# Reading neighbourhood values straight from the normed values, a lasting weight slot, and other queues and buffers at the turn from projection to scan

## The chip, the cores and the metric

The kernel runs on one core of a Trainium2 chip. The metric is the device time of one execution in microseconds (us); smaller is better. Before the change the median of three runs is 1549.68 us (1549.65 to 1550.4). The change is a set of edits around the moment at which the kernel goes from its input projection to its scan and attention.

## The reference

One layer of a hybrid backbone: 256 context tokens and 1024 latent tokens of width 1024. After a normalisation with learned shift and scale, one projection feeds two groups of heads. Group A is a gated DeltaNet: a five-tap convolution over the sequence and SiLU on q, k and v, and then a scan over chunks, forward and backward. Group B is an attention of every latent token to a window on a 2-D grid 64 wide, and to the context. Both go through one output projection, and a SwiGLU network follows. Cut to what the change touches:

```python
qkv = short_conv(p[..., :3 * DN_WIDTH], conv_w)          # convolution, then SiLU
q, k, v = split(qkv)                                      # DeltaNet, 4 heads of 128
z = p[..., 3 * DN_WIDTH:4 * DN_WIDTH]                     # output gate
o = rms_norm(scan_forward(q, k, v) + scan_backward(q, k, v)) * silu(z)
nq, nk, nv = na_qkv(p)                                    # attention, 8 heads of 64, q and k normed
# each latent query: one softmax over its window keys (12 grid rows x 32 columns a block)
# plus the 256 context keys; values are gathered from nv in the same window
```

## The kernel before

**Staging.** The projection is a list of jobs (L1030 to 1041) that all read the same 1280-token input, held in SBUF (on-chip memory) as pairs `hh`, `hl`. A Block job makes 128 output channels: 24 groups of three matmuls (L405) into three PSUM banks, a copy out by ScalarE (L453), the convolution on VectorE (L457 to 461), SiLU (L468), and a `finish` that norms, splits or transposes and stores to DRAM. A Wide job makes 256 channels with the tokens on the partitions (L595), its weights in a slot `zw`. The order is k0 to k3, z's second half (z1), nk0 to nk2, the first half of the attention's values (nv0), nk3, q0 to q3, nq0 to nq3, v0, nv1, v1 to v3, and z's first half (z0). Beside the jobs run background generators: the inverses of the chunks' triangular matrices, the preparation of chunks (`preps`, which stores `y_d` and `at_d`, L1010), and the modulation vectors. With z0 the attention begins (`fill`, L1064 to 1068); then scan and attention run interleaved, and after them the output projection and the feed-forward network.

**What sets the order.** An automatic scheduler orders the instructions of every engine at build time; at run time each engine takes them strictly in that order, and each waits for what it needs. DMAs are issued in the same in-order streams of SyncE (SP) or ScalarE (ACT). The framework gives the DMAs of a program a set of eight completion semaphores in turn, so an issue also waits until the DMA eight places before it has landed. Tiles live in stacks on the left and right of SBUF; a tile that is put over an older one waits for the last reader of the old one.

**What the change touches.**

- `values` (L276 to 281) loads for each of 32 attention pairs a tile `vw`, 192 KB, from `vw_d`. That DRAM tensor is a rearranged copy of `nv_d`, made after nv1 by 64 DMAs of 64 KB from DRAM to DRAM on SP (L1103 to 1109).
- `Block.finish` for v stores `vt` to `v_d` on SP (L535). The scan loads `v` from `v_d` (L1165).
- Wide jobs: z1, nv0 and nv1 take `zw` from the pool `zp`, which belongs to `late`, the pools that close before z0; z0 takes it from `sp1`, a new pool that is opened only once `late` is closed (L1061 to 1068). Each slot is filled in two halves through one landing tile `wraw`: load (L586), cast by ScalarE (L587), rest by GpSimd (POOL, L588). `sp1` later holds the scan's output `oacc` in the same slot.
- z0 gathers its gate tile `zg` (L624) under the tag `kx` of the pool `cp`, stores it by ACT's queue (L627).
- `norm` of nk and nq: per segment of tokens one matmul (L492) into a bank and one Ln by ScalarE (L493); nk has three segments. The bank comes from the tag `m`; the tag `pr` serves `preps`.
- `mneg`, two masks times -1e30, is made at the start of the kernel.
- The scan's pools on the right stack: `sl` (loads `kt`, `y`, `kT`, `qT`, `at`), then a pad, then `sw` (work tiles and `v`).

## Time and profile before

| | us |
|---|---|
| median of three runs | 1549.68 |
| the profiled execution's own time | 1549.54 |
| its span, first to last instruction | 1547.5 |
| TensorE (PE) busy | 1479.8 |
| VectorE (DVE) busy | 994.3 |
| ScalarE (ACT) busy | 727.7 |
| GpSimd (POOL) busy | 233.6 |
| mean granted TensorE clock | 0.982 |

Times in the trace are us from the start of the span. In a row of the timeline stand start, duration, engine, line, operation, output<-input, how many, and in brackets the idle time before it and what ended it. SPq and ACTq are the queues on which SP and ACT issue DMAs: such a row shows the time of issuing, not of the transfer. A row of the windows gives for a stretch its length, then busy time and instruction count of PE, PE's weight loads, DVE, ACT and POOL, then the granted TensorE clock, the mean busy share of the 16 DMA engines and GB/s.

### The profile page before, as it was taken

What the parts mean: (1) busy time and instruction counts of PE and PEld (TensorE: products, weight loads), DVE (VectorE), ACT (ScalarE), POOL (GpSimd) and SP (SyncE); (2) the same over time, 40 slices, a digit from 0 to 9 for tenths busy, and PEclk for the clock granted to TensorE, in tenths of its full rate; (3) what the DMA queues carried; (4) which work ended last, traced back from release to release, by engine and by line L of the source; (5) the groups of instructions that cost most, each with busy time, mean ns of one, the idle gap of its engine ahead of it and who ended that gap; (6) DMA issues with size and microseconds to landing.
All of it is one profiled execution on the core that took longest, in us unless ns stands there. A gap on an engine that the chain in (4) does not pass through costs nothing. (4 is left out here: it accounts for less than half of the span.)

```text
span 1547.5 us, 23963 instructions
## 1 busy us (share of the span) xinstructions
PE 1479.8 (96%) x8702; PEld 1235.2 (80%) x8702; DVE 994.3 (64%) x1712; ACT 727.7 (47%) x1404; POOL 233.6 (15%) x286
## 2 busy tenths in 40 slices
PE   6999999899989978999999999999999999999998
PEld 3788787678778867888887878888888888888887
DVE  5774497675554543777986469866665556599652
ACT  5442552635764235666773166333333334354440
POOL 1154500733554010111210000000000000000000
PEclk9999999999999979999999999999999999999999
DMA  9274221577556467899637502632323324698742
GB/s 389 64 217 133 67 72 63 163 212 241 182 169 212 130 174 237 283 288 261 220 102 255 208 34 82 211 102 103 103 102 103 109 100 159 231 381 279 244 144 82
DMA packets 204118, 267.35 MB, mean 173 GB/s; under 512 B 16736, under 2 KB 114528, under 8 KB 202976
## 3 DMA queue, kind: packets, MB, share of 16 engines
q1 hardware_dynamic: 198480, 261.07, 51.7%
q10 hardware_dynamic: 5520, 4.76, 0.9%
q8 instruction: 68, 1.11, 0.3%
q14 instruction: 50, 0.41, 0.1%
HBM read 201.02 MB, written 68.94 MB: 174 GB/s over the span
## 5 line engine op out<-in xcount | busy, mean ns | idle before, releaser
L405 PE MATMUL blk<-hh,whi 128*128 128x512 f32 (+1 forms) x410 | 123.4, 395 | 2.3 <-ACT kk L550 1.4
L1415 ACT CAST uhi<-wq 128x512 fp32r<-128x512 f32 x101 | 61.0, 622 | 133.5 <-issue 84.6
L1415 ACT CAST uhi<-ws 128x512 fp32r<-128x512 f32 x91 | 53.9, 621 | 147.3 <-PE ps L1354 92.9
L405 PE MATMUL blk<-hl,whi 128*128 128x512 f32 (+1 forms) x410 | 116.8, 377 | 0.3 <-DVE hl L707 0.3
L595 PE MATMUL blk<-zw,hh 128*128 128x256 f32 (+1 forms) x576 | 115.0, 293 | 1.3 <-ACT kk L550 1.1
L405 PE MATMUL blk<-hh,wlo 128*128 128x512 f32 (+1 forms) x410 | 114.7, 377 | 0.6 <-POOL wlo L200 0.6
L1416 DVE TENSOR_TENSOR ulo<-wq,uhi 128x512 fp32r<-128x512 f32 x101 | 67.4, 687 | 59.1 <-ACT uhi L1415 34.0
L1354 PE MATMUL ps<-hT,uhi 128*128 128x512 f32 x336 | 103.7, 390 | 0.0
L1354 PE MATMUL ps<-hT,ulo 128*128 128x512 f32 x336 | 103.5, 389 | 0.0
L1354 PE MATMUL ps<-lT,uhi 128*128 128x512 f32 x336 | 103.4, 389 | 0.0
L595 PEld LDWEIGHTS blk<-zw,hh 128*128 128x128 f32 x576 | 92.8, 192 | 5.2 <-ACT kk L550 1.4
L1354 PE MATMUL ps<-hB,uhi 128*128 128x512 f32 x288 | 89.2, 391 | 0.6 <-ACT hB L1529 0.6
L1354 PE MATMUL ps<-lB,uhi 128*128 128x512 f32 x288 | 88.7, 389 | 0.4 <-DVE lB L1530 0.4
L1354 PE MATMUL ps<-hB,ulo 128*128 128x512 f32 x288 | 88.7, 389 | 0.0
L405 PEld LDWEIGHTS blk<-hh,wlo 128*128 128x128 f32 x410 | 72.6, 192 | 15.3 <-POOL wlo L200 0.9
L405 PEld LDWEIGHTS blk<-hl,whi 128*128 128x128 f32 x410 | 72.4, 191 | 14.5 <-DVE hl L707 0.8
L405 PEld LDWEIGHTS blk<-hh,whi 128*128 128x128 f32 x410 | 69.4, 194 | 18.2 <-issue 4.5
L595 PE MATMUL blk<-zw,hl 128*128 128x256 f32 (+1 forms) x288 | 83.2, 289 | 0.0
L1354 PEld LDWEIGHTS ps<-lT,uhi 128*128 128x128 f32 x336 | 63.1, 188 | 13.1
L1354 PEld LDWEIGHTS ps<-hT,ulo 128*128 128x128 f32 x336 | 63.1, 188 | 13.1
L1354 PEld LDWEIGHTS ps<-hT,uhi 128*128 128x128 f32 x336 | 62.9, 188 | 13.0
L200 POOL TENSOR_TENSOR wlo<-wraw,whi 128x1024 fp32r<-128x1024 f32 x18 | 44.7, 2485 | 179.2 <-ACT whi L199 160.7
(359 smaller groups left out, 3540.5 us busy)
## 6 DMA issues: line engine op xcount, KB each, us to landing
wq<-w_fo SPq DMA_DIRECT2D x99, 256.0 KB, 4.2
wq<-w_gu SPq DMA_DIRECT2D x88, 256.0 KB, 2.9
wad<-wa SPq DMA_DIRECT2D x64, 256.0 KB, 4.4
bt<-rpb SPq DMA_DIRECT2D x64, 192.0 KB, 3.8
t_d<-g SPq DMA_DIRECT2D x22, 512.0 KB, 3.6
fr<-t_d SPq DMA_DIRECT2D x44, 256.0 KB, 5.0
f_d<-g SPq DMA_DIRECT2D x33, 256.0 KB, 2.1
fr<-f_d SPq DMA_DIRECT2D x33, 256.0 KB, 3.8
```

The costliest lines, as they stand in the source:

```text
L200: lo_engine.tensor_tensor(o, r, h.bitcast(F32), OP.subtract)
L405: pe.matmul(o, ww[:, k], xx[k][:, s], start=k == 0 and j == 0, stop=k == KT - 1 and j == 2)
L595: pe.matmul(p[:, :c1 - c0], x[k][:, s], ww[:, k, c0:c1], start=k == 0 and j == 0, stop=k == KT - 1 and j == 2)
L1354: pe.matmul(o, w[wi][:, k], x[xi][:, k], start=first and k == 0 and j == 0, stop=k == n - 1 and j == 2, skip_group_check=True)
L1415: act.copy(hi, self.raw[key])
L1416: dve.tensor_tensor(lo, self.raw[key], hi.bitcast(F32), OP.subtract)
```

## The change

Five edits:

1. The copy `nv_d` to `vw_d` goes. `values` reads `nv_d` itself, by four DMAs of 48 KB (32 partitions each, in pieces of 512 B) where it had one of 192 KB.
2. The four v blocks' stores to `v_d` go out on ACT's queue.
3. All four Wide jobs take `zw` from one slot of `sp1`, which is opened before `late`, and z0's weights can so be fetched like any other; `zg` takes the tag `cr` for `kx`.
4. The third segment of nk's norm takes its bank from `pr`; `mneg` moves to the pool `adp`, and its two multiplications behind the masks' arrival.
5. In the scan's right-hand stack `sw` now comes first, then the pad, then `sl`, and `v` is an `sl` tile; the loaded tiles thereby lie over the convolution's buffers.

```diff
@@ values, L276
             vw = nw.tile([128, 3, 128], F32, name="vw", tag="vw", bufs=3)
-            sp.dma_start(vw, vw_d[:, hp, cb, half:half + 3])
+            for r in range(4):
+                rows = nv_d[CT:].rearrange("(n r c) d -> r c n d", r=4, c=64)[r, BLKS[cb]:BLKS[cb] + 32, half:half + 3]
+                sp.dma_start(vw[r * 32:r * 32 + 32], rows[:, :, hp * 128:hp * 128 + 128])
@@ Block.norm, L490
-                for s0, n in self.segs:
-                    p = bank()
+                for j, (s0, n) in enumerate(self.segs):
+                    p = bank("pr" if j == 2 else "m")
@@ Block.finish, L535
-                    sp.dma_start(dst[:, i * 128:(i + 1) * 128].rearrange("(c p) d -> p c d", p=128), vt)
+                    (act if kind == "v" else sp).dma_start(dst[:, i * 128:(i + 1) * 128].rearrange("(c p) d -> p c d", p=128), vt)
@@ Wide, L574
-                w = self.zp().tile([128, 2, KT, 256 if self.lasting else 272], F32R, name="zw", tag="zw")
+                w = sp1.tile([128, 2, KT, 272], F32R, name="zw", tag="zw")
-                if not self.lasting:
-                    self.room()
+                self.room()
-                            zg = cp.tile([128, NCH, 128], F32, name="zg", tag="kx", bufs=3)
-                            zg = zg.rearrange("p a b -> p (a b)")[:, :1024]
+                            zg = cp.tile([128, T], F32, name="zg", tag="cr", bufs=2)
+                            zg = zg[:, :1024]
@@ masks and pools, L756
-                        for d in range(2):
-                            act.mul(mneg[:, d], masks[:, d], -1.0e30)
+        sp1 = pools(middle, "sp1", "left")
         adp = pools(late, "adp", "left")
-        zpool = [pools(late, "zp", "left")]
+        mneg = adp.tile([128, 2, 128], F32R, name="mneg", tag="mneg")
+        for d in range(2):
+            act.mul(mneg[:, d], mr[:, d].bitcast(F32), -1.0e30)
@@ before z0, L1061
                 late.close()
-                sp1 = pools(middle, "sp1", "left")
-                zpool[0] = sp1
-                jobs[n + 1].room()
@@ after nv1, L1103
-            if isinstance(j, Wide) and n == values:
-                vlat = nv_d[CT:].rearrange("(r c) d -> r c d", c=64)
-                for cb in range(4):
-                    for ch in range(4):
-                        for r in range(4):
-                            sp.dma_start(vw_d[r * 32:r * 32 + 32, :, cb, ch],
-                                         vlat[4 * ch + r, BLKS[cb]:BLKS[cb] + 32].rearrange("c (h d) -> c h d", d=128))
@@ scan, L1143
-        sl = pools(gs, "sl", "right", 3)
+        sw = pools(gs, "sw", "right", 2)
         shift(gs, "spad", "right", 16)
-        sw = pools(gs, "sw", "right", 2)
+        sl = pools(gs, "sl", "right", 3)
@@ load, L1164
-                t = work(name, 3) if name == "v" else sl.tile([128, 4, 128], F32, name=name, tag=name)
+                t = sl.tile([128, 4, 128], F32, name=name, tag=name)
```

The edits also make the scheduler order the engines anew. Three places of that order follow; a row holds line (the change's lines lie 2 to 4 above those of before in this region, 14 in the scan), operation, output<-input, shape and count.

**From the last chunks to the start of z0.** SP before: `vw_d` is the copy, `at_d` and `y_d` the last chunks' stores, `wraw<-w_z` the two halves of z0's weights, `qs`, `kh`, `kl`, `vc`, `bt` and `vw` the attention's loads.

```order
L1108 DMA vw_d<-nv_d 128x128 x53
L1010 DMA at_d<-at 128x512 x2
L1010 DMA y_d<-y_2229 128x512
L1010 DMA y_d<-y_2230 128x512
L1010 DMA y_d<-y_2231 128x512
L1010 DMA y_d<-y_2232 128x512
L586 DMA wraw<-w_z 128x8x128
L535 DMA v_d<-vt 128x10x128
L260 DMA qs<-nq_d 128x1024
L262 DMA kh<-nk_d 64x1280
L263 DMA kl<-nk_d 64x1280
```

SP with the change:

```order
L1006 DMA at_d<-at 128x512 x2
L1006 DMA y_d<-y_2228 128x512
L1006 DMA y_d<-y_2229 128x512
L584 DMA wraw<-w_z 128x8x128
L1006 DMA y_d<-y_2231 128x512
L1006 DMA y_d<-y_2230 128x512
L584 DMA wraw<-w_z 128x8x128
L258 DMA qs<-nq_d 128x1024
L260 DMA kh<-nk_d 64x1280
L261 DMA kl<-nk_d 64x1280
L260 DMA kh<-nk_d 64x1280
L261 DMA kl<-nk_d 64x1280
```

The 53 copies are gone, the second half of the weights is issued ahead of the attention's loads and not 15 rows behind the first, and no store of `v_d` stands between. PE there, before: the end of v3 (L405) and the first rows of the attention (L303, scores of the first pair).

```order
L405 MATMUL blk<-hh_458,wlo 128x256
L405 MATMUL blk<-hh_458,wlo 128x512 x2
L303 LDWEIGHTS qs
L303 MATMUL sc<-kh,qs 128x256
L303 LDWEIGHTS qs
L303 MATMUL sc<-kh,qs 128x256
```

PE with the change:

```order
L405 MATMUL blk<-hh_456,wlo 128x256
L405 MATMUL blk<-hh_456,wlo 128x512 x2
L593 MATMUL blk<-zw,hh_127 128x256
L593 MATMUL blk<-zw,hl_128 128x256
L593 MATMUL blk<-zw,hh_127 128x256
L593 MATMUL blk<-zw,hh_129 128x256
L593 MATMUL blk<-zw,hl_130 128x256
```

z0's matmuls (L593) now follow v3 directly. Past 96 matmuls of it come the transposes for v's store and only then the first scores:

```order
L593 MATMUL blk<-zw,hl_457 128x256
L593 MATMUL blk<-zw,hh_456 128x256
L527 MATMUL m<-cst,cacc 128x128 x4
L303 LDWEIGHTS qs
L303 MATMUL sc<-kh,qs 128x256
L303 LDWEIGHTS qs
L303 MATMUL sc<-kl,qs 128x256
```

**The third segment of nk3.** PE before (L492 is the norm's matmul; the L405 rows ahead of it end the block q0, those behind belong to q1):

```order
L405 MATMUL blk<-hl_459,whi 128x512 x2
L405 MATMUL blk<-hh_458,wlo 128x512 x2
L492 MATMUL m<-cr,cst 128x256
L492 MATMUL m<-cr,cst 128x512
L405 MATMUL blk<-hh_129,whi 128x512 x2
L405 MATMUL blk<-hl_130,whi 128x512 x2
L492 MATMUL m<-cr,cst 128x512
L405 MATMUL blk<-hh_129,wlo 128x512 x2
```

PE with the change; the third matmul doesn't follow the second:

```order
L405 MATMUL blk<-hl_457,whi 128x512 x2
L405 MATMUL blk<-hh_456,wlo 128x512 x2
L492 MATMUL m<-cr,cst 128x256
L492 MATMUL m<-cr,cst 128x512
L405 MATMUL blk<-hh_127,whi 128x512 x2
L405 MATMUL blk<-hl_128,whi 128x512 x2
L405 MATMUL blk<-hh_127,wlo 128x512 x2
```

It comes 87 rows on, behind the last rows (L994) of the first two chunks' preparation, whose banks have the same tag, and within q2:

```order
L994 MATMUL pr<-y_2230,kk 32x96
L994 MATMUL pr<-y_2231,kk 32x96
L994 MATMUL pr<-y_2230,kk 32x96
L994 MATMUL pr<-y_2231,kk 32x96
L405 MATMUL blk<-hh_454,whi 128x512 x2
L405 MATMUL blk<-hl_455,whi 128x512
L492 MATMUL pr<-cr,cst 128x512
L405 MATMUL blk<-hl_455,whi 128x512
L405 MATMUL blk<-hh_454,wlo 128x512 x2
```

**The last store of v.** ACT before, from the last copy out of z0 (L624) to the attention's next copies; SP issues the store of v3 meanwhile:

```order
L624 COPY zg<-blk 128x256
L626 ACT_TABLE_LOAD
L626 ACTIVATE zg<-zg 128x1024
L317 COPY pt<-sc 128x640
L627 DMA z_d<-zg 128x4x256
L317 COPY pt<-sc 128x640
L307 ACT_TABLE_LOAD
L307 ACTIVATE bt,mx<-bt,mx 128x640 x2
L326 COPY no<-sc 128x8x16
```

ACT with the change:

```order
L622 COPY zg<-blk 128x256
L624 ACT_TABLE_LOAD
L624 ACTIVATE zg<-zg 128x1024
L317 COPY pt<-sc 128x640
L625 DMA z_d<-zg 128x4x256
L317 COPY pt<-sc 128x640
L307 ACT_TABLE_LOAD
L307 ACTIVATE bt,mx<-bt,mx 128x640 x2
L535 DMA v_d<-vt 128x10x128
L326 COPY no<-sc 128x8x16
```

The store of `v_d` stands behind the silu of z's gate, a table load and two exponentials of the attention.

More of the change, by code (lines that the diff above doesn't have):

```diff
@@ L137, in hybrid @@
     mr = const("mr", [128, 5, 128], F32R)
-    mneg = const("mneg", [128, 2, 128], F32R)
     v_d = dram.tile([T, 512], F32, name="v_d", tag="v_d")
@@ L149, in hybrid @@
     nk_d = dram.tile([2, NAH, ND, T], F16, name="nk_d", tag="nk_d")
-    vw_d = dram.tile([128, 4, 4, 4, 128], F32, name="vw_d", tag="vw_d")
     y_d = dram.tile([2, NCH, 128, 4, 128], F32, name="y_d", tag="y_d")
@@ L564, in hybrid, with __init__ @@
         class Wide:
-            def __init__(self, kind, half, zp):
-                self.kind, self.half, self.zp = kind, half, zp
+            def __init__(self, kind, half):
+                self.kind, self.half = kind, half
                 self.n = 272 if kind == "z" and half else 256
-                self.lasting = kind == "z" and not half
             def room(self):
-                w = self.zp().tile([128, 2, KT, 256 if self.lasting else 272], F32R, name="zw", tag="zw")
+                w = sp1.tile([128, 2, KT, 272], F32R, name="zw", tag="zw")
                 self.hi, self.lo = w[:, 0], w[:, 1]
@@ L767, in hybrid @@
         KKc = WK[:, 1]
-        def zp():
-            return zpool[0]
         def decay_tables(gp):
@@ L1028, in preps @@
                 flush(tick[0] + 2)
-        jobs = first + [Block("k", 2), Block("k", 3), Wide("z", 1, zp)]
+        jobs = first + [Block("k", 2), Block("k", 3), Wide("z", 1)]
         inv = len(jobs)
-        jobs += [Block("nk", i) for i in range(3)] + [Wide("nv", 0, zp), Block("nk", 3)]
+        jobs += [Block("nk", i) for i in range(3)] + [Wide("nv", 0), Block("nk", 3)]
         turn = len(jobs)
@@ L1036, in hybrid @@
         queries = range(turn, later)
-        jobs += [Block("nq", i) for i in range(4)] + [Block("v", 0), Wide("nv", 1, zp)]
+        jobs += [Block("nq", i) for i in range(4)] + [Block("v", 0), Wide("nv", 1)]
         values = len(jobs) - 1
-        jobs += [Block("v", i) for i in (1, 2, 3)] + [Wide("z", 0, zp)]
+        jobs += [Block("v", i) for i in (1, 2, 3)] + [Wide("z", 0)]
         def blk(n):
@@ L1142, in hybrid @@
     with ExitStack() as gs:
+        sw = pools(gs, "sw", "right", 2)
+        shift(gs, "spad", "right", 16)
         sl = pools(gs, "sl", "right", 3)
-        shift(gs, "spad", "right", 16)
-        sw = pools(gs, "sw", "right", 2)
         gs.callback(scan_psum.close)
```

## The prediction

> **What bounds the kernel now.** I read the page first, then the windows around the places where PE idles, then PE's waits there, and last the queue that feeds them. The page says that PE is nearly always busy, and that the chain that ended last is PE's:
>
> ```profile
> span 1547.5 us, 23963 instructions
> PE 1479.8 (96%) x8702; PEld 1235.2 (80%) x8702; DVE 994.3 (64%) x1712; ACT 727.7 (47%) x1404; POOL 233.6 (15%) x286
> ...
> PE 41%; DVE 1%; issue 0%; DVEq 0%
> ```
>
> So 1547.5 - 1479.8 = 67.7 us are PE's idle time, and an edit that removes no matmul can win only from these and from matmuls that ran at a lower granted clock. The windows show where (length, then busy time of PE, PEld, DVE, ACT, POOL, the clock, DMA share, GB/s):
>
> ```profile
> 200.00:258.00 58.00, 52.48 (x348) 46.34 (x346) 55.62 (x56) 23.29 (x34) 5.46 (x2) 1.00 0.22 64
> ...
> 258.00:300.00 42.00, 37.79 (x184) 30.20 (x183) 25.71 (x21) 22.96 (x39) 22.42 (x27) 0.87 0.54 182
> 300.00:344.00 44.00, 40.63 (x261) 32.55 (x259) 28.44 (x30) 20.01 (x35) 15.70 (x15) 0.89 0.53 159
> ...
> 495.88:531.97 36.09, 36.09 (x262) 29.20 (x261) 14.06 (x20) 12.66 (x26) 4.68 (x9) 1.00 0.38 112
> ...
> 548.50:563.38 14.88, 3.93 (x19) 2.24 (x19) 12.70 (x17) 6.63 (x10) 2.57 (x2) 0.63 1.06 294
> 563.38:569.50 6.12, 5.98 (x29) 5.50 (x28) 3.05 (x6) 2.03 (x5) 2.39 (x2) 0.51 0.50 139
> 569.50:595.04 25.54, 25.49 (x218) 24.38 (x217) 4.55 (x9) 8.12 (x14) 0.31 (x1) 1.00 0.36 98
> 595.04:607.16 12.12, 8.57 (x60) 6.69 (x58) 6.13 (x13) 10.25 (x15) 0.93 (x3) 0.72 1.01 308
> ...
> 600.00:800.00 200.00, 194.47 (x1824) 171.28 (x1825) 151.80 (x461) 142.31 (x389) 33.40 (x68) 0.98 0.81 251
> 820.00:1547.50 727.50, 722.24 (x3198) 596.55 (x3196) 471.38 (x745) 288.35 (x488) 0.00 (x0) 1.00 0.47 160
> ```
>
> From 820 on PE lacks 5 us of 727, and the change edits nothing there: what is won or lost before 820 goes to the end at full value. The one deep hole lies between the last matmul of v3 (548.5) and the first of z0 (563.38). What PE waited for from 545 to 610, and when z0 began, ended and the scan's first product ran:
>
> ```profile
> PE sc L303 <- DVE mx L305: 5.1, 2, 4.1
> PE sc L303 <- DMA kh<-nk_d: 4.5, 1, 4.5
> PE sc L314 <- DVE bt L309: 3.0, 2, 2.3
> ...
> 563.38 0.56 PE L595 MATMUL blk<-zw,hh 128*128 128x256 f32 x1
> ...
> 595.04 0.38 PE L527 MATMUL m<-cst,cacc 128*128 128x128 f32 x2
> ...
> 607.16 1.13 PE L1217 MATMUL ps<-v,y 128*128 128x128 f32 x8 [0.66 <-DMA y<-y_d]
> ```
>
> The causes stand in SP's queue:
>
> ```profile
> 495.88 36.09 SPq L1108 DMA_DIRECT2D vw_d<-nv_d  x53
> 532.07 1.01 SPq L1010 DMA_DIRECT2D at_d<-at  x2
> 533.18 2.42 SPq L1010 DMA_DIRECT2D y_d<-y  x4
> 535.68 0.61 SPq L586 DMA_DIRECT2D wraw<-w_z  x1
> 545.47 0.37 SPq L535 DMA_DIRECT2D v_d<-vt  x1
> 545.93 0.63 SPq L260 DMA_DIRECT2D qs<-nq_d  x1
> ...
> 555.34 0.60 SPq L586 DMA_DIRECT2D wraw<-w_z  x1
> ...
> 596.43 0.39 SPq L535 DMA_DIRECT2D v_d<-vt  x1
> ...
> 602.13 0.32 SPq L1165 DMA_DIRECT2D v<-v_d  x1
> ```
>
> The 53 copies keep SP for 36 us; then the store of v1 waits until 545.47 for its data with the attention's loads right behind it, and the second half of z0's weights comes last, at 555.34. So PE has neither scores nor z0 to work on. It waits 4.5 us for `kh`, 4.1 us for the first pair's bias step, which stands on DVE behind v3's convolution, and 2.3 us for the pair's softmax.
>
> **The change part by part. The hole before z0** (edits 1 to 3). With the copies and the v store out of SP's stream, the second half of z0's weights is issued behind the last chunks' stores and needs its landing tile only. I put it near 530, since nothing but those chunks holds it, instead of 555.34; the lasting slot removes the wait for the pools' closing. In PE's order z0 follows v3 directly, and 96 matmuls of it run before the first scores, which gives DVE time for v3's convolution. What can be recovered: idle 14.88 - 3.93 = 10.95, 6.12 - 5.98 = 0.14 and 25.54 - 25.49 = 0.05, so 11.1 us; slow clock 3.93 x (1 - 0.63) = 1.5 and 5.98 x (1 - 0.51) = 2.9, so 4.4 us. Together 15.5 us. Against it stand new waits, which this trace doesn't show: z0's first bank is released by ScalarE's copies of v3, at most the 1.35 us of the first row below; the two casts of z0's weights now stand around v2's copies in ScalarE's order and may hold the banks of v2, at most two of the second row, 2.1 us; and the first pair's softmax may keep PE for the 2.3 us that it takes now. Each may as well be 0, since z0 leaves PE other work. I take half of their 5.8, 2.9 us: **12.6 us won**, between 9.7 and 15.5.
>
> ```profile
> 548.13 1.35 ACT L453 COPY cr<-blk 128x256 f32<-128x256 f32 x3 [5.77 <-PE blk L405]
> 549.35 1.07 ACT L587 CAST zw<-wraw 128x1024 fp32r<-128x1024 f32 x1
> ```
>
> **nk's third segment** (edit 4). Four waits for the bank, and the times of nk3's third Ln and of the last copy (L1001) of the first two chunks' preparation:
>
> ```profile
> PE m L492 <- ACT cr L493: 5.3, 4, 1.4
> ...
> 274.51 0.69 ACT L493 ACTIVATE cr<-m,bias 128x512 f32<-128x512 f32 x1 [0.64 <-PE m L492]
> ...
> 320.43 0.47 ACT L1001 COPY y<-pr 32x384 f32<-32x384 f32 x1 [2.14 <-PE pr L998]
> ```
>
> Two of the waits lie in 200 to 258, where DVE is busy 55.62 of 58 us: the inverses' chain on DVE takes up what PE gains there. The other two are worth 2.7 us. But for nk3 the order shows the third product behind those chunks' preparation, so its Ln goes from 274.5 to about 320, and ACT loads its tables twice more. Behind it queue nk3's Exp, its store, and the release of its tiles to q0's squares and q1's convolution. Who waits? The sums and products of q0 and q1, which the order moves back; PE gets the blocks q2 and q3 instead. From 258 to 344 there are 4.2 + 3.4 = 7.6 us idle before. Upper bound: 2.7 and half of that, 6 us won. Lower bound: the pushed-back products find no cover and cost as much as half the idle time and two table loads (1.28 us each by the row below), about 5 us lost with the two waits not regained. I take **2 us won**, nearer the gain, because PE's own matmuls need nothing from nk3.
>
> ```profile
> 595.63 1.28 ACT L626 ACT_TABLE_LOAD   x1
> ```
>
> **The scan's start** (edits 2 and 5). The loads over the convolution's buffers no longer wait for z0's last matmul, but that wait decides nothing before: the first load, `v`, waits for v3's store (596.43, `v` at 602.13), and `kt`, `y`, `kT` are queued behind it. The store now stands on ACT behind the last silu, the store of z, two copies, a table load and two exponentials. By the trace of those same instructions, which run from 595.24 to 602.98 before, it goes out some 7 us after the end of z0's last products where it took 1.4, so the first scan product comes up to 18 us behind them, not 12.1. PE has more of the attention to run meanwhile: in its order 8 us of products stand ahead of the first scan row against 5, at the durations that they have at full clock, 3 us more. That is 5.6 - 3 = 2.6 us lost; if ACT gets there early, as its casts and copies now lie further ahead, 3 us are won of the 12.12 - 8.57 = 3.6 idle and 8.57 x 0.28 = 2.4 slow. I take **1.5 us lost**, nearer the queue's arithmetic.
>
> ```profile
> 595.24 0.37 ACT L624 COPY zg<-blk 128x256 f32<-128x256 f32 x1 [2.76 <-PE blk L595]
> ...
> 602.98 0.19 ACT L307 ACTIVATION_READ_ACCUMULATOR bt<-bt,mx 128x1 f32 x1
> ```
>
> **Four loads for one** (edit 1). 32 loads become 128, so 96 more issues and the same 6.3 MB, in 600 to 800:
>
> ```profile
> bt<-rpb SPq DMA_DIRECT2D x64, 192.0 KB, 3.8
> ...
> vw<-vw_d SPq DMA_DIRECT2D x32, 192.0 KB, 3.6
> ...
> 640.44 0.32 SPq L278 DMA_DIRECT2D vw<-vw_d  x1
> ...
> 679.29 0.35 SPq L1165 DMA_DIRECT2D y<-y_d  x1
> ```
>
> Each costs SP at least the 0.32 us above: 96 x 0.32 = 31 us of some 200. Between the last two rows SP issues 49 DMAs in 38.9 us, so about half its time is free, and 7 of them are `vw`, which makes 21 more. Pieces of 512 B cost the engines little: the copies moved such pieces, and 36.09 us there at a share of 0.38 with 112 GB/s is 295 GB/s at a full share, against 251 / 0.81 = 310 in the scan. PE is 97% busy there, and loads run a pair ahead. Bounds: 0, and all of PE's idle time there once more, 200 - 194.5 = 5.5. I take **2 us lost**, between them. The copies' traffic and 64 issues, which hid behind PE's full 36.09 us of 36.09, win nothing by themselves.
>
> The Trainium skill (DMA: Bandwidth & Descriptors, Rules for kernel authors) speaks against this edit: coalesce, since transfers under 64 KB are mostly overhead; its Bandwidth table gives 0.95 us of DMA time for 64 KB. By that, an estimate, 128 x 0.95 = 122 us would stand where 32 larger ones took less than half, and the scan would be bound by its DMAs. The row of the copies contradicts it where several are under way: 53 in 36.09 us at a share of 0.38 is 0.26 us each. The sum doesn't use it.
>
> **Sum.** 12.6 + 2 - 1.5 - 2 = 11.1 us. The profiled execution took 1549.54 us, 2.04 of it outside the span; less 11.1 it is 1538.4. The median lies 0.14 above the profiled one: **1538.6 us**. The edit of `mneg` and `zg`'s tag I cost at nothing: two multiplications move behind the masks on an engine that is idle half the time.
>
> **The rivals.** *Most comes back, and more.* The scan's start wins its 3, nk its 6, the extra loads cost nothing: 12.6 + 6 + 3 = 21.6, or 1528 us. For it: the start is bound by late loads, all of which move forward but one. Against: that one is first in the queue. Chance 0.13.
>
> *The wait moves on.* The holes close before z0, but nk3's late norm costs its 5 and the store of v3 its 2.6: 12.6 - 5 - 2.6 - 2 = 3.0, or 1546.7 us. For it: ACT is 10.25 of 12.12 us busy at the scan's start. Against: nothing of nk3 feeds PE's blocks. Chance of a result from 1543 to 1546.6, by this or half of it, 0.17.
>
> *Slower: the DMA stream falls behind.* An issue waits for the DMA eight places before it. In the stretch of 49 issues in 38.9 us this allows 8 x 38.9 / 49 = 6.4 us of landing time each; with 21 more it allows 8 x 38.9 / 70 = 4.4. The medians are 3.6 to 3.8 us. From 4.4 on the stream decides: at 5 us the stretch lasts 70 x 5 / 8 = 43.8, 4.9 longer, and the 200 us of the phase 25 longer. With the other terms as above that is 1549.7 - 13.1 + 25 = 1561.6 us; from 4.7 us on it takes more than they win. For it: the DMA share of 0.81 and the medians' nearness. Against: a DMA of 48 KB has a quarter of the bytes to land. Chance of slower 0.09. The skill's rule on small transfers points this way. *That the holes stay* (the second half of the weights is late for another reason, such as its landing tile) would give no change: 0.06, with the mixtures near it.
>
> **How the numbers follow.** The forecast (1530 to 1543) has 0.55, and the rivals 0.13, 0.17, 0.06 and 0.09. 0.2%, or 3.1 us, is what a measurement of this kernel can tell from no change: faster 0.85, same 0.06, slower 0.09. The range of 1529 to 1547 leaves out about 0.07 below and 0.13 above.
>
> **What would show it.** Right: z0's first matmul within 2 us of v3's last, a clock of 1.00 from 548 to z0's end, which comes 10 to 15 us earlier; nk3's third Ln near 320 with no new wait of PE over 2 us up to 344; the first scan product 12 to 18 us behind the last of z0. Wrong: waits of PE on `vw` or `bt` between 600 and 800, a stretch from the scan's first product to 820 that is over 5 us longer, or a PE wait for banks around 320.

## The result and the profile after

The change makes the kernel slower: 1563.99 us, the median of four runs (1561.9 to 1567.58), against 1549.66 before; the ratio is 1.0094 with a 95% interval of 1.0073 to 1.0116. The profiled execution has a span of 1563.8 us. The forecast was 1538.6 us, with a range of 1529 to 1547. One of the eight executions of run x13 below fell into a slower state of the chip (1665.19 us at a granted clock of 0.846) and is left out of its median.

The first half of the forecast is in the trace. These are windows of the changed kernel, from v3's end to z0's end, and from there to the first product of the output projection (w_out); columns as before:

```profile
548.50:579.50 31.00, 30.30 (x260) 29.04 (x261) 16.32 (x30) 11.54 (x23) 0.62 (x2) 1.00 0.38 111
...
579.40:829.00 249.60, 221.32 (x1964) 190.24 (x1962) 168.12 (x491) 158.01 (x426) 34.83 (x70) 0.94 0.69 212
```

The hole is gone. PE is busy 30.30 of 31 us at full clock, z0 begins at 549.07 (it began at 563.38) behind one wait for v3's copies, and its last product starts at 579.4 where it started at 594.9 ("z0's end" below is this start). That is 15.5 us won:

```profile
549.07 0.39 PE L593 MATMUL blk<-zw,hh 128*128 128x256 f32 x1 [1.03 <-ACT cr L453]
```

Then more than all of it is lost. The same window of the kernel before, from z0's end to the output projection:

```profile
594.90:813.70 218.80, 209.51 (x1963) 183.37 (x1961) 162.79 (x491) 156.58 (x425) 34.14 (x71) 0.98 0.77 239
```

The same matmuls take 249.6 us instead of 218.8, so 30.8 us are lost. 249.6 - 221.3 = 28.3 us of the new window are idle, where 9.3 were, which makes 19.0; and the matmuls themselves are 11.8 us longer, at a mean clock of 0.94 where it was 0.98. The part of the clock is not a fixed price: x2 and x3 below have the order of the changed kernel's products in this window but for a few rows, and there the products are 11.3 and 6.6 us longer. From here on "the stretch" is this window, from the last product of z0 to the first of the output projection. Behind it both kernels run alike (734.8 us to the end of the span after, 733.8 before).

The biggest single gap of the stretch, in PE's timeline and in SP's queue of the changed kernel:

```profile
751.53 0.37 PE L303 MATMUL sc<-kh,qs 128*128 128x256 f16 x1 [5.71 <-DVE mx L305]
```

```profile
736.38 0.42 SPq L1151 DMA_DIRECT2D qT<-qT_d  x1
736.85 0.43 SPq L258 DMA_DIRECT2D qs<-nq_d  x1
737.33 0.45 SPq L260 DMA_DIRECT2D kh<-nk_d  x1
742.58 0.33 SPq L1151 DMA_DIRECT2D at<-at_d  x1
743.47 0.32 SPq L1151 DMA_DIRECT2D kt<-k_d  x1
743.84 0.69 SPq L261 DMA_DIRECT2D kl<-nk_d  x1
...
745.86 0.59 SPq L283 DMA_DIRECT2D vc<-nv_d  x1
746.55 0.88 SPq L270 DMA_DIRECT2D bt<-rpb  x2
747.49 1.84 SPq L278 DMA_DIRECT2D vw<-nv_d  x4
```

PE waits for a pair's bias step on DVE, which needs the bias `bt`. The bias is issued at 746.55, behind the scan's load `at`. That load had to wait until 742.58 for its buffer, with everything behind it standing still. The bias lands 3.7 us after its issue, at 750.25, while the scores that it is added to were done at 736.6; DVE is then at the end of a row of small steps of the scan, and starts the bias step at 750.65. So a late bias is not a slow transfer here; it is an issue at the back of an in-order queue.

How SP waits in the whole stretch, changed kernel first, then the kernel of the first experiment below (x1, one load a pair); the columns are the total, how often, and the longest:

```profile
SPq L1151 <- PE ps L1215: 15.9, 5, 4.7
SPq L1151 <- PE ps L1203: 13.6, 6, 3.7
...
SPq L1151 <- PE ps L1220: 9.4, 6, 3.9
```

```profile
SPq L1151 <- PE ps L1203: 12.2, 13, 1.3
...
SPq L1151 <- PE ps L1215: 7.0, 11, 1.0
SPq L1151 <- PE ps L1220: 6.0, 7, 1.3
```

L1151 is the scan's loads, and the releasers are the products that free their buffers. With four loads these waits are fewer, and the longest of a row lasts 2.8 to 4.7 times as long. What changed is where the loads stand in SP's order. A chunk's loads there, changed kernel and x1 (row texts as the order has them):

```text
changed: at, y, at | bt x2, vw x4, bt x2, vw x4, bt, vw x3, bt, vw | v, kt, y, kT, qT, at, v, y ...
x1:      kh, qT, bt, vw, kl, y, bt, v, y, bt, kT, at, qT, z, kt, vw, at, kt, bt, z, bt ...
```

Counted over the whole program, the number of scan loads that stand ahead of the first bias of each of the 32 pairs:

```text
changed: 0 0 0 0 0 21 22 22 33 34 34 46 46 58 58 58 62 62 62 74 74 86 86 86 86 86 98 98 98 98 98 98
x1:      0 0 0 0 0 21 22 25 30 33 40 43 49 54 56 64 64 65 68 72 76 83 86 89 92 94 96 97 98 98 98 98
before:  0 0 0 0 10 21 21 25 30 33 40 42 49 53 56 63 64 65 68 71 76 83 86 89 92 94 96 97 98 98 98 98
```

With one load a pair the scheduler mixes the scan's loads and the attention's one by one. With four it lays all loads of a chunk, up to 12, in a block ahead of the next pair's biases.

How late the biases come can be worked out from the traces. For each of the 32 pairs, take the time from the last product of its first scores to the landing of its first bias, where that is positive. The columns are the pairs with more than 1 us, the sum over all pairs, and the longest:

| run | late pairs | sum us | longest us |
|---|---|---|---|
| before | 3 | 11.0 | 6.2 |
| changed kernel | 11 | 61.6 | 13.6 |
| x1 one load | 2 | 5.7 | 3.4 |
| x4 before, load split | 13 | 66.9 | 12.3 |
| x5 tiny loads | 2 | 5.5 | 3.2 |
| x10 scan loads on GpSimd's queue | 1 | 1.5 | 1.5 |
| x11 blocks of 6 | 11 | 44.1 | 8.5 |
| x13 one load, blocks forced | 15 | 91.7 | 13.9 |

These sums are not time lost, since PE has other work while a pair waits. They show which kernels have late biases: those with the blocks in SP's order.

### The profile page after: what moved, and what is told of

Its sections match the earlier page's. It is cut to its first block, busy times and chain, and to the rows that moved or that the text cites. A ratio compares the mean times of both kernels' runs of the same rounds, so it can differ in the third digit from the quotient of the medians.

```text
span 1563.8 us, 23965 instructions
## 1 busy us (share of the span) xinstructions
PE 1486.8 (95%) x8702; PEld 1239.0 (79%) x8702; DVE 997.7 (64%) x1712; ACT 730.2 (47%) x1405; POOL 236.6 (15%) x286
## 5 line engine op out<-in xcount | busy, mean ns | idle before, releaser
L405 PE MATMUL blk<-hh,whi 128*128 128x512 f32 (+1 forms) x410 | 122.3, 391 | 4.6 <-ACT cacc L438 1.8
L405 PE MATMUL blk<-hl,whi 128*128 128x512 f32 (+1 forms) x410 | 115.6, 375 | 0.3 <-DVE hl L705 0.3
L593 PE MATMUL blk<-zw,hh 128*128 128x256 f32 (+1 forms) x576 | 112.6, 289 | 2.0 <-ACT cr L453 1.0
L405 PE MATMUL blk<-hh,wlo 128*128 128x512 f32 (+1 forms) x410 | 113.1, 371 | 0.6 <-POOL wlo L198 0.6
L593 PEld LDWEIGHTS blk<-zw,hh 128*128 128x128 f32 x576 | 91.0, 189 | 4.8 <-ACT cr L453 1.5
L405 PEld LDWEIGHTS blk<-hh,whi 128*128 128x128 f32 x410 | 69.4, 191 | 20.7 <-issue 4.0
L405 PEld LDWEIGHTS blk<-hl,whi 128*128 128x128 f32 x410 | 72.0, 191 | 14.3 <-DVE hl L705 0.8
L405 PEld LDWEIGHTS blk<-hh,wlo 128*128 128x128 f32 x410 | 71.4, 190 | 14.7 <-POOL wlo L198 0.9
L593 PE MATMUL blk<-zw,hl 128*128 128x256 f32 (+1 forms) x288 | 81.8, 284 | 0.0
L1340 PEld LDWEIGHTS ps<-hT,ulo 128*128 128x128 f32 x336 | 63.1, 188 | 13.1
L1340 PEld LDWEIGHTS ps<-lT,uhi 128*128 128x128 f32 x336 | 63.1, 188 | 13.1
```

The source lines that it names most:

```text
L405: pe.matmul(o, ww[:, k], xx[k][:, s], start=k == 0 and j == 0, stop=k == KT - 1 and j == 2)
L593: pe.matmul(p[:, :c1 - c0], x[k][:, s], ww[:, k, c0:c1], start=k == 0 and j == 0, stop=k == KT - 1 and j == 2)
L1340: pe.matmul(o, w[wi][:, k], x[xi][:, k], start=first and k == 0 and j == 0, stop=k == n - 1 and j == 2, skip_group_check=True)
```

## The experiments

| run | median us | ratio to before | 95% interval | stretch us |
|---|---|---|---|---|
| before | 1549.66 | | | 218.8 |
| changed kernel | 1563.99 | 1.0094 | 1.0073 to 1.0116 | 249.6 |
| x1 one load | 1540.22 | 0.9937 | 0.9916 to 0.9958 | 223.9 |
| x2 pools back | 1564.06 | 1.0091 | 1.0061 to 1.0122 | 253.2 |
| x3 bank back | 1563.16 | 1.0082 | 1.0053 to 1.0111 | 246.5 |
| x4 before, load split | 1577.41 | 1.0171 | 1.0125 to 1.0217 | 246.5 |
| x5 tiny loads | 1548.85 | 0.9999 | 0.998 to 1.0018 | 232.2 |
| x6 loads on GpSimd's queue | 1548.91 | 0.9993 | 0.9974 to 1.0012 | 227.7 |
| x7 two loads | 1541.4 | 0.9945 | 0.9918 to 0.9972 | 226.8 |
| x8 staged, rows outermost | 1584.94 | 1.0214 | 1.0172 to 1.0257 | 225.5 |
| x9 staged, columns outermost | 1558.8 | 1.0067 | 1.0042 to 1.0092 | 222.8 |
| x10 scan loads on GpSimd's queue | 1549.15 | 1.0002 | 0.9978 to 1.0026 | 231.3 |
| x11 blocks of 6 | 1558.97 | 1.0062 | 1.0039 to 1.0085 | 241.0 |
| x12 x9 with v on SP | 1554.89 | 1.0041 | 1.0022 to 1.006 | 219.5 |
| x13 one load, blocks forced | 1560.18 | 1.0079 | 1.0055 to 1.0104 | 242.2 |
| x14 x9 with v on GpSimd | 1553.03 | 1.0028 | 1.0008 to 1.0047 | 216.7 |
| x15 x9 with copies on ACT | 1541.11 | 0.9953 | 0.9932 to 0.9974 | 223.8 |

The stretch is read from the one profiled execution of each run. The changed kernel, x2 and x3 have the same order of products in it but for a few rows, and read 249.6, 253.2 and 246.5, so differences in the stretch of under some 7 us are not read. The ratios are to executions of the kernel before that were taken together with the run's own.

**x1: one load for four.**

```diff
-            for r in range(4):
-                rows = ...[r, BLKS[cb]:BLKS[cb] + 32, half:half + 3]
-                sp.dma_start(vw[r * 32:r * 32 + 32], rows[:, :, hp * 128:hp * 128 + 128])
+            rows = nv_d[CT:].rearrange("(n p) d -> p n d", p=128)
+            rows = rows[:, half:half + 3, hp * 128:hp * 128 + 128]
+            sp.dma_start(vw, rows)
```

> The changed kernel with one load of 192 KB for each pair's values in place of four of 48 KB; it reads other rows of nv_d, so that the values in the windows are wrong, with the same bytes in the same pieces of 512 B. Theory A (the four loads lengthen SP's in-order stream in the scan, and with it the attention's loads come late): the stretch from the end of z0 to the first product of the output projection (L1317) falls from 249.6 us back toward the 218.8 of before, and the time to 1535 to 1542. Theory B (the scan's pools and what their tiles wait for): 1560 to 1566, no change. Theory C (the attention's earlier start re-orders scan and attention for the worse, whatever the loads): 1555 to 1566.

Measured: 1540.22 us, the stretch 25.7 us shorter than in the changed kernel. Theory A holds: the loss goes with the four loads. The other four edits then win some 10 us by the ratio (6.5 to 13.0), where the prediction's sum had 13.1 for them. The pieces of 512 B are still there, and the stretch is 5 us above that of before, so they cost little.

**x2: the scan's pools as before.**

```diff
-        sw = pools(gs, "sw", "right", 2)
-        shift(gs, "spad", "right", 16)
         sl = pools(gs, "sl", "right", 3)
+        shift(gs, "spad", "right", 16)
+        sw = pools(gs, "sw", "right", 2)
```

> The changed kernel with the scan's pools in the order of before (sl, pad, sw, and v in sw). The order of PE's instructions stays the same, so only waits on tiles can change. Theory A: within 3 us of the changed kernel's 1564. Theory B: the pools' waits cost the scan its 31 us, so 1533 to 1545. Theory C: within 3 us of 1564.

Measured: 1564.06 us. Theory B falls: the loss doesn't depend on where the loads' buffers lie.

**x3: nk's third segment in the bank `m`.**

```diff
-                    p = bank("pr" if j == 2 else "m")
+                    p = bank()
```

> The changed kernel with nk's third segment back in the bank m. All theories of the scan put the loss behind z0, so the time stays within 4 us of 1564; z0's end, at 579.4 in the changed kernel, shows what the bank is worth: the prediction's 2 us won means an end near 581, its lower bound an end near 574.

Measured: 1563.16 us, and z0 ends at 581.4, 2 us later than in the changed kernel. But in x2, whose order up to z0 is that of the changed kernel, it ends at 575.2. So two executions of the same order differ by 4 us there, and the 2 us of the bank are inside that.

**x4: the kernel before with its load in four.**

```diff
-            sp.dma_start(vw, vw_d[:, hp, cb, half:half + 3])
+            for r in range(0, 128, 32):
+                sp.dma_start(vw[r:r + 32], vw_d[r:r + 32, hp, cb, half:half + 3])
```

> The kernel before with each load of a pair's values cut into four of 32 partitions, still from vw_d, nothing else. Theory A: the scan and attention (218.8 us from the end of z0 to the output projection's first product) lose 25 to 35 us, time 1572 to 1585. Theories B and C: within 5 us of 1549.7.

Measured: a ratio of 1.0171, 1577.41 us against 1551.6 for the kernel before in the same runs, and a stretch 27.7 us longer. The four loads cost the same in a kernel that has none of the other edits. Its SP order has the same blocks (46, 46, 58, 58, 58, 62, ...).

**x5: as many issues, x1's order.**

```diff
             sp.dma_start(vw, rows)
+            few = nw.tile([32, 3, 2], F32, name="few", tag="few", bufs=1)
+            for r in range(3):
+                sp.dma_start(few[:, r], rows[r * 32:r * 32 + 32, 0, :2])
```

> x1_one_load with three tiny loads more for each pair (32 rows of 8 bytes into a tile that nobody reads), so that SP issues as many DMAs as in the changed kernel. The order of every instruction on PE, DVE and ACT is the same as in x1. Theory A1 (the number of issues on SP's in-order queue costs the time): 1560 to 1568, like the changed kernel. Theory A2 (the scheduler, planning with four loads, puts PE, DVE and ACT in another order, and that order costs it): 1537 to 1545, like x1. In between, both have a part.

Measured: 1548.85 us, the stretch 8.3 us longer than x1's. So the number of issues has a part, at most about a third of the loss, and the rest goes with something that the tiny loads don't change: the order of PE, DVE and ACT is that of x1, and the biases come as early as in x1. The 8.3 us are an upper figure for the issues. In 5.0 of them PE's products run longer at a lower clock (0.96 for 0.98), and SP waited 6.3 us for earlier tiny loads to land in their one buffer, which the four loads don't do.

**x6: the four loads on GpSimd's queue.**

```diff
-                sp.dma_start(vw[r * 32:r * 32 + 32], rows[:, :, hp * 128:hp * 128 + 128])
+                pool.dma_start(vw[r * 32:r * 32 + 32], rows[:, :, hp * 128:hp * 128 + 128])
```

> The changed kernel with the four loads, complete and of the right rows, issued by GpSimd's queue. PE, DVE and ACT have the order of x1. Theory A1 (SP's issues): 1537 to 1545, since SP is rid of all of them. Theory A2 (the order): also 1537 to 1545. Were the transfers themselves at fault (128 of 48 KB instead of 32 of 192 KB), it would stay at 1555 to 1566.

Measured: 1548.91 us, no different from before, with a stretch of 227.7. The 128 transfers of 48 KB themselves show as 3.8 us over x1's stretch, within what is not read. The median is 4 us above the expected range, and z0 ended at 582.6; why the stretch's gain doesn't show in full is not settled.

**x7: two loads of 64 partitions.**

```diff
-            sp.dma_start(vw, rows)
+            for r in (0, 64):
+                sp.dma_start(vw[r:r + 64], rows[r:r + 64, half:half + 3, hp * 128:hp * 128 + 128])
```

> x1_one_load with two loads of 64 partitions a pair (wrong rows as there, same bytes). PE, DVE and ACT stand nearly in x1's order. Theory A1: a third of the way from x1 to the changed kernel, 1546 to 1550. Theory A2: 1538 to 1543.

Measured: 1541.4 us. The loss doesn't grow evenly with the issues: two loads cost nearly nothing, four cost all. That is how a re-ordering looks, not a price per issue, and SP's order is in fact mixed as in x1 (43, 49, 55, 56, 58, 61 scan loads ahead where the changed kernel has 46, 46, 58, 58, 58, 62).

**x8: a copy in 16 DMAs.**

```diff
+            if isinstance(j, Wide) and n == values:
+                for cb in range(4):
+                    for ch in range(4):
+                        sp.dma_start(vw_d[:, :, cb, ch].rearrange("(r c) h d -> r c h d", r=4), ...)
```

> The changed kernel with the copy of the values back, but made by 16 DMAs of 256 KB on SP in place of 64 of 64 KB, and one load of 192 KB a pair: the other four edits stand, the result is complete. If the hole before z0 closes because SP is held for 16 short issues (about 10 us) and not for 64, and the scan costs what it does with one load: 1535 to 1543, faster than before. If the copies hold SP as long as before (36 us, because of their bytes): 1545 to 1552.

Measured: 1584.94 us, far outside. SP's queue in it:

```profile
501.38 65.94 SPq L1099 DMA_DIRECT2D vw_d<-nv_d  x15
```

Each copy of 256 KB held SP for 4.4 us, at a DMA share of 0.25, so the attention's first load came at 573 and PE waited 31.9 us for `kh`. The outermost dimension of these copies has 4 elements, and a quarter of the 16 engines is what the share shows. The Trainium skill (DMA: Bandwidth & Descriptors, Rules for kernel authors) says so: an outermost dimension of fewer than 16 confines a DMA to at most that many engines. x9 agrees from the other side: 32 outermost, 12.71 us for 16 copies, 0.8 us each, at a DMA share of 0.92.

**x9: the copy with the 32 columns outermost.**

```diff
+                for cb in range(4):
+                    for r in range(4):
+                        sp.dma_start(vw_d[r * 32:r * 32 + 32, cb], vlat[r, BLKS[cb]:BLKS[cb] + 32])
```

> The changed kernel with a copy of the values again, in 16 DMAs of 256 KB whose outermost dimension is the 32 columns (x8 had the 4 rows outermost, and 15 of them held SP for 65.9 us), and one load of 192 KB a pair. The result is complete. Theory A (the hole before z0 and the four loads are separate; one load keeps the scan's and attention's loads finely mixed in SP's order): the copies hold SP 10 to 16 us, done before the last chunks, so 1537 to 1544, faster than before by 5 to 13 us. Rival (any copy on SP brings the hole back): 1547 to 1552.

Measured: 1558.8 us, above the ranges of both theories. The stretch is right (222.8), but z0 ends at 596.4: the hole is back, though SP had issued the copies by 507.5. SP's waits between 505 and 560, and its queue:

```profile
SPq L583 <- DMA v_d<-vt: 22.6, 1, 22.6
```

```profile
494.77 12.71 SPq L1099 DMA_DIRECT2D vw_d<-nv_d  x16
...
548.69 0.60 SPq L583 DMA_DIRECT2D wraw<-w_z  x1
```

The first half of z0's weights waited 22.6 us for the store of v1. That store is on ACT's queue, where it stood until its data came (issued at 544.97). SP's and ACT's DMAs share eight completion semaphores in the trace, and the store and this load have the same one. A store that was moved off SP so as not to hold it up holds it up through the semaphore: the attention's first loads come late with the weights, and PE waits 8.1 us for `kh`. But this wait alone doesn't make z0 late. In ACT's order of x9 the cast of the first half of the weights stands behind v3's SiLU, at 557.16, 4.6 us after the load had landed (552.6); in the changed kernel the two casts stand at 523.07 and 531.25. x14 below shows what that order does without the coupling.

**x10: the scan's loads on GpSimd's queue, four loads on SP.**

```diff
-                sp.dma_start(fl(t), src)
+                pool.dma_start(fl(t), src)
```

> The changed kernel, four loads of the values on SP, with the scan's own loads (v, kt, y, kT, qT, at) issued by GpSimd's queue instead of SP's. PE's order is within 113 of 7776 instructions of x1's, against 842 in the changed kernel. Theory A3 (the loss of some 14 us beside the issues comes from SP's order: blocks of 12 scan loads, each waiting for its buffer, stand ahead of the next pair's biases and values): the waits for late biases go, 1540 to 1550. Theory A1 (issues alone, on any queue): 1555 to 1566.

Measured: 1549.15 us, the stretch 18.3 us shorter than the changed kernel's, with the same four loads on the same queue. A3 holds, A1 falls as the whole cause. The scheduler's order of PE is back near x1's as well (58 of the stretch's 1961 products stand otherwise, against 385 in the changed kernel), so this run alone doesn't tell SP's order from the order of the other engines.

**x11: blocks of 6.**

```diff
-            if i + 1 < NCH:
-                for d in range(2):
-                    load(d, ORDER[d][i + 1], ORDER[1 - d][i + 2:i + 3])
+            todo = [0, 1] if i + 1 < NCH else []
...
+                for d in todo[:1]:
+                    load(d, ORDER[d][i + 1], ORDER[1 - d][i + 2:i + 3])
+                todo = todo[1:]
```

> The changed kernel with the second direction's scan loads called one step of the scan later, so that in SP's order blocks of 6 scan loads stand ahead of a pair's biases in place of 12; as many issues on SP. Theory A3: a gain of some 4 to 10 us on the changed kernel, 1554 to 1560. Theory A1: no gain, 1560 to 1568.

Measured: 1558.97 us, the stretch 8.6 us shorter than with blocks of 12, at the same number of issues, and the biases less late. Two blocks of 10 and 12 are left in SP's order, and 5.6 of the 8.6 us are a higher clock (0.99), so the size of the gain is uncertain.

**x12: x9 with the stores of v on SP.**

```diff
-                    (act if kind == "v" else sp).dma_start(dst[...], vt)
+                    sp.dma_start(dst[...], vt)
```

> x9 with the stores of v back on SP's queue: it shows what that edit is worth. The prediction had ACT's late store of v3 cost 1.5 us at the scan's start, but SP's store of v1 waits until about 545 with the attention's loads and the second half of z0's weights behind it. If that wait brings the hole back: 6 to 14 us slower than x9. If the copies alone made the hole: within 2 us of x9.

Measured: 1554.89 us, not slower than x9, so neither expectation came: the hole is there in both. The store of v1 stands on SP until 544.80, with the attention's loads right behind it, the second half of the weights goes out at 560.49, and z0 ends at 597.4. The first half had left at 525.91, but its cast stands at 557.01 in ACT's order, behind v3's SiLU as in x9, and the second half waited another 5.8 us for the landing tile that this frees. So the run doesn't show what the store on SP costs by itself.

**x13: x1 with the blocks forced.**

```diff
+    def behind(ld, scan=False):
+        begun.extend([1] * scan)
+        if line and begun:
+            tc.add_manual_dep(ld.ins, line[-1].ins.name, ...NoSync..., reason="program order")
+        line.append(ld)
...
-                sp.dma_start(bt[:, w0:w0 + 384], ...)
+                behind(sp.dma_start(bt[:, w0:w0 + 384], ...))
...
-                sp.dma_start(fl(t), src)
+                behind(sp.dma_start(fl(t), src), True)
```

> x1_one_load (one load a pair, wrong rows) with the scan's loads and the biases' loads held to the order in which the program names them, by edges that order SP's issues and wait for nothing on the chip. SP's order then has the blocks of 12 scan loads ahead of a pair's biases that the changed kernel has, with a third fewer issues; PE, DVE and ACT are re-planned around it. Theory A3 (the blocks in SP's order make the biases late): 1550 to 1558, most of the way from 1540 to the 1557 that the changed kernel would have without its issues. Theory A1 (issues alone): 1538 to 1543.

Measured: 1560.18 us, above the expected range, with one load a pair. The stretch is 18.3 us longer than x1's. This is the strongest run: no load was split, and the loss is there as soon as SP's order has the blocks, nearly the same ones as in the changed kernel (34, 46, 46, 58, 58, 58, 62 scan loads ahead of the biases), and the biases are late. With the 8.3 us of x5 it makes 26.6, and x1 lies 25.7 below the changed kernel; that the two add up so well is partly luck. In idle time of PE they make 16.9 + 3.5 = 20.4 us against 14.7, the rest is clock, and by the ratios they make 22 + 10 = 32 us against 24. The forced order also re-planned PE, DVE and ACT: 507 of the 1961 products stand otherwise than in x1, and 454 otherwise than in the changed kernel. So the same blocks cost much the same under a third order of the engines, but no run has them under x1's. SP stands still at the scan's loads in few and long waits again, in the row below 6 of up to 3.8 us where x1 has 7 of up to 1.3; its longest waits are here for the buffers of values and biases, up to 6.2 us:

```profile
SPq L1160 <- PE ps L1229: 12.0, 6, 3.8
```

**x14: x9 with the stores of v on GpSimd's queue.**

```diff
+                    if kind == "v":
+                        for h in (0, 5):
+                            pool.dma_start(to[:, h:h + 5], vt[:, h:h + 5])
```

> x9 with the stores of v on GpSimd's queue, in two halves each. In x9 the first half of z0's weights waited 22.6 us on SP for the store of v1, which ACT had issued but could not start until 545: eight DMAs on, it shares its completion semaphore. GpSimd's DMAs use others. If that coupling brought x9's hole back: the hole closes, 1538 to 1545. If the copies did, or GpSimd's other work is held up behind its store: 1549 to 1558.

Measured: 1553.03 us. The coupling is gone, the first half of the weights goes out at 523.70 and the attention's loads at 524.40. But SP then stands 24.7 us for the landing tile of the weights, which GpSimd frees once ACT has cast the first half, and the second half goes out at 559.12, so z0 still ends at 596.4:

```profile
SPq L588 <- POOL zw L590: 24.7, 1, 24.7
```

```profile
554.46 1.27 ACT L467 ACTIVATE cacc<-cacc 128x1280 f32<-128x1280 f32 x1 [7.87 <-DVE cacc L460]
555.63 1.03 ACT L589 CAST zw<-wraw 128x1024 fp32r<-128x1024 f32 x1
```

The weights had long landed. ACT's order has their cast behind v3's SiLU (the first row), and that waits for the convolution on DVE. So x9's hole doesn't need the coupling of the queues: the order that the scheduler chose for ACT is enough.

**x15: x9 with the copies on ACT.**

```diff
-                        sp.dma_start(vw_d[r * 32:r * 32 + 32, cb], vlat[r, BLKS[cb]:BLKS[cb] + 32])
+                        act.dma_start(vw_d[r * 32:r * 32 + 32, cb], vlat[r, BLKS[cb]:BLKS[cb] + 32])
```

> x9 with the 16 copies issued by ACT. SP's order up to the attention's first loads is then like the changed kernel's, with z0's weights ahead of the last chunks' stores. ACT is held some 12 us by 15 copies at about 500, ahead of its copies of v1's banks. If x9's hole came from the order of issues and their semaphores: the hole closes, less up to 6 us of PE's wait for banks at 500, 1540 to 1548. If any copy brings the hole back: 1550 to 1558.

Measured: 1541.11 us, 0.9953 of before (0.9932 to 0.9974), complete, and faster than both kernels. ACT issues the copies, both halves of the weights leave SP ahead of the attention, and ACT casts them at 524.30 and 533.14:

```profile
502.21 8.99 ACTq L1099 DMA_DIRECT2D vw_d<-nv_d  x13
```

```profile
520.01 0.60 SPq L583 DMA_DIRECT2D wraw<-w_z  x1
528.29 0.59 SPq L583 DMA_DIRECT2D wraw<-w_z  x1
```

z0 ends at 583.3, and the stretch is 223.8.

## Why the prediction was wrong

**What bounds the kernel: right.** In the changed kernel nothing behind the stretch took more than 1 us, so what happened ahead of it went to the end at full value, the loss as well as the gain.

**The hole before z0: right, and a little too careful.** 12.6 us were forecast, with 2.9 us of new waits. From 548.5 to z0's end it was 46.4 us before, and 30.9 in the changed kernel: 15.5, the upper bound, of which up to 0.5 is v3's earlier end. The one new wait that shows was the 1.03 us for v3's copies. The second half of the weights went out at 527.13, forecast near 530. Which of the edits closed it is not separated. Every kernel here that copies on SP has the hole (before, x4, x8, x9, x12, x14), with the store of v on SP, ACT or GpSimd; x15, which copies on ACT, has not. The prediction looked for the causes in SP's queue. In x9, x12 and x14 a second condition shows, the place of the weights' casts in ACT's order. The prediction saw the casts move forward, but counted them only as a possible cost.

**nk's third segment: not resolved.** Its Ln came at 315.17, forecast about 320, and no wait of PE of over 2 us followed up to 344 (the longest was 1.3). The 2 us are within what executions of one order differ by at z0's end. Two of the term's bounds were summed wrongly, which changes nothing: 2.7 and half of 7.6 are 6.5, not 6, and half of 7.6 and two table loads are 6.4, not 5.

**The scan's start: right.** The last store of v left at 585.95, 6.5 us behind z0's end, forecast some 7; the first scan product came at 597.45, 18 us behind it, forecast up to 18. PE idles 5.1 us there where it idled 3.6, and the lower clock costs 2.5 as before, so some 1.5 us are lost, as forecast.

**Four loads for one: this is the step that failed.** The prediction took "2 us lost, between them", with 0 and 5.5 as bounds. It priced the issues (96 of 0.32 us) against SP's free time (six of the DMAs that it counted there are `vw`, not seven), and the transfers against the engines' rate, and it bounded the loss by PE's idle time of before. The stretch lost 30.8 us, of which some 1.5 are the scan's start. The transfers were indeed cheap: a load landed in 2.7 us by the row below, against 3.6 for one of four times its size, and x6 leaves them at most 3.8 us. The issues alone cost up to 8.3 (x5), more than the bound; why so much is not shown. The larger part has to do with neither: some 18 us, whether the order is forced on one load (x13) or the scan's loads are taken out of the queue (x10). The scheduler, planning with four loads, put SP's loads into another order, and in that order each chunk's loads, which wait for their buffers, stand ahead of the next biases. The first bias of 11 pairs then lands over 1 us after its scores, by up to 13.6 us, where one load a pair has two such pairs. How much of the loss the new order of PE, DVE and ACT adds by itself is open. The prediction took for granted that 96 more issues would be 96 more rows between the old ones. It read SP's order at z0 and not in the scan, where the blocks stand. One of its own signs of being wrong came: from the scan's first product to the output projection it took 231.5 us instead of 206.6.

```profile
vw<-nv_d SPq DMA_DIRECT2D x128, 48.0 KB, 2.7
```

**The slower rival: right in sign, and near in time by another route.** It gave 1561.6 us, from landing times of 5 us at eight DMAs in flight, and held 0.09. Landing times fell, so its mechanism did not happen, and that its time is near is luck. The rule of the Trainium skill (DMA: Bandwidth & Descriptors, Rules for kernel authors) that transfers under 64 KB are mostly overhead, which was weighed beside it, does not explain the loss either (x6). "The wait moves on" named ACT and nk, and neither lost what it was to lose.

The working was wrong in its bounds as well: a loss was bounded by idle time that PE already had, as though a wait could not be new. And a slower clock came on top: 11.8 of the 30.8 us are the same matmuls at a lower granted clock. Why the clock was lower is open: in x13 PE idles 30.5 us of the stretch, and its matmuls are only 2.2 us longer than before, at a clock of 0.99. One place of the changed kernel is the window behind the gap of 5.71 us:

```profile
750.00:760.00 10.00, 7.18 (x41) 4.63 (x41) 6.09 (x20) 6.33 (x17) 3.52 (x4) 0.57 0.94 251
```

## What to carry to other kernels

A DMA that is split into more is not only that many issues more. It changes what the scheduler finds free, and with it the order of the in-order queue; read that order where the extra issues fall, and look for loads that wait for a buffer standing ahead of loads that somebody needs soon. Two streams with different releases (here the scan's buffers and the attention's biases) belong finely mixed in one queue, or in two queues. And undo one part of a change of five: here four of the edits together were worth some 10 us (x1) and one cost some 24.

## What the runs showed that was not expected

- Queues are coupled by completion semaphores: in x9 an issue on SP stood 22.6 us for a store on ACT's queue, eight DMAs ahead, that had itself to wait for its data. GpSimd's DMAs use eight others, and x14 has no such wait. The changed kernel has a smaller case of it, 5.8 us at `kl`, hidden behind z0.
- Fetching weights early is worth nothing when the engine that casts them has the cast late in its order: in x14 they left at 523.70 and were cast at 555.63.
- A DRAM-to-DRAM copy of 256 KB held its queue 4.4 us with 4 elements outermost, at a DMA share of 0.25, and 0.8 us with 32.
- The stretch takes two loads a pair for next to nothing (226.8 us against 223.9) and four for 25.7 us.
